# Hybrid SSD block on one core: gate weights split beside the pairs and kept as two parts, z tiles moved into a pair, rows of x loaded and scaled one by one

## The chip, the cores and the metric

The kernel runs on one core of one Trainium2 chip. The metric is device time in microseconds (us) of that core, lower is better. Engines are called by the names of the profile: PE multiplies matrices, PEld loads its weights, DVE and ACT are the vector and the scalar engine, POOL is GpSimd, SP only issues DMAs. ACT and POOL also issue DMAs, each on a queue of its own.

## The reference

One block of a streaming encoder on x of 1024 rows by 1024 channels, all float32. Cut to what matters:

```
h = rmsnorm(x) * norm_mix_w
z, xbc, dt, s_b, s_c, s_x, g_a, g_b = split(h @ w_in)     # 2048, 3072, 32, then five of 1024
xs, B, C = split(silu(causal_conv4(xbc) + bias))
y = scan over chunks of (xs, softplus(dt), A, B, C) + D * xs  # 32 heads in 4 groups
y = group_rmsnorm(y * silu(z)) * ssd_norm_w
a = y @ w_ssd_proj
b = (s_b * causal_conv3(s_c * s_x)) @ w_sconv_proj
x = x + (sigmoid(g_a) * a + sigmoid(g_b) * b) @ w_o
x = x + (silu(n @ w_gate) * (n @ w_up)) @ w_down,  n = rmsnorm(x) * norm_ffn_w
out = rmsnorm(x) * final_norm_w
```

## The kernel before, in words

**Arithmetic.** Every large product is made of three PE instructions. An operand is split into a high part (a copy by ACT into a rounded type) and a low part (a DVE subtraction of the high part from the original); then high times high, high times low and low times high are added in PSUM. One such instruction has 128 rows, 128 columns of weights and 512 columns of data. Most products are also made by a seven-product scheme (Strassen's, in Winograd's form) on halves: a `Pair` (line 834) is two slabs of w_in, 128 columns each, and its seven products each take 4 steps in depth times 3 instructions, 84 in all. A tile that is made without the scheme takes 2 halves of rows times 8 steps times 3, 48 instructions.

**Memory.** Nearly all tiles in SBUF are 47 equal pages of 128 x 1024 float32 (`page`, line 60). A page is given out again when its last user is done, and the instruction that writes it next waits for that. There are 8 PSUM banks.

**Order.** The schedule is written by hand: the order of the Python calls is the order of each engine's instructions, and every queue runs in order. Generators are advanced by one step at chosen places, so that their work lies between other work.

1. **Head** (lines 226 to 258 and 1530 to 1604). Rows of x come as eight tiles of 128 rows. Tiles 0 and 2 are loaded on SP's queue, 1 and 3 on ACT's, 4 to 7 later on ACT's (`more_loads`). Constants come on POOL's queue, and after them the first weight slabs. ACT and DVE make the sums of squares of tiles 0 to 3 in turn (`rows_sq_on`), then one norm for all four (`rstd_of`, a chain of seven small instructions, one of them on ACT), then the scaled rows in two halves of columns (`rows_scale(..., parts=2)`: DVE takes three tiles, ACT one). PE turns the scaled rows (32 transposes of 128 x 128, `turn_rows`, each group of four into one bank), ACT and DVE take the banks out (`turned_out`), `put` splits them, and `p0.pe(1)` is the first real product (line 1580). `wdt_split` and `steps_pe` make the first part of the time steps, then come the first products of two more pairs and the second half of the rows.
2. **Pairs** (lines 1641 to 1701). 31 pairs, 217 slots (a slot is one product of one pair, 12 PE instructions). A slot's evictions (`ev`), the preparation of later slots (`make`), loads about 11 slots ahead (`load_pairs`, on SP), one step of the side work (`pump`: convolutions, silu), and on every third slot a step of `all_weight_sums`, which adds blocks of later weights in DRAM with POOL's accumulating DMAs.
3. **Direct tiles beside the scans** (lines 961 to 1016). 18 tiles without the scheme: z tiles 14 and 15, and the 16 gate tiles of g_a and g_b. For each, SP loads the slab two tiles ahead, ACT makes the high part (`direct_hi`) and DVE the low part (`direct_lo`) one tile ahead. Among their PE instructions lie the 65 steps of the scan (`scans`, 32 items of two steps), spread evenly over the tiles by `turn` and `SCAN_STEPS`. The norms of y ride on the scan's steps.
4. **Two projections and the output projection** by the scheme, with chunks loaded and split ahead (`Stream`), then the **FFN**. In its `second_half` (line 1192) the turned rows of the second half are combined: two subtractions at lines 1209 and 1212, one generator step apart, each followed by the split of two pages.

The loop over the direct tiles, with the lines that the change takes out or edits:

```
for hf in range(2):
    ps = bank("pr")
    for k in range(KT):
        mm3(ps, wh[:, k, :], wl[:, k, :], bh, bl, k == 0, k == KT - 1)
        ...
        if i + 1 < len(direct) and (hf, k) == (0, 1):
            direct_hi(direct[i + 1][0])
        if i + 1 < len(direct) and (hf, k) == (0, 7):
            direct_lo(direct[i + 1][0])
        if i + 2 < len(direct) and (hf, k) == (0, 2):
            direct[i + 2][0].load()
    ev(ps, hf)
```

Of the kernel before, what the change touches and what calls it, by code (L numbers as in the profile page):

```python
# [8 lines left out]
F32 = mybir.dt.float32  # L9
# [4 lines left out]
P = 128  # L14
# [25 lines left out]
def hybrid_block(ctx: ExitStack, tc: tile.TileContext, x, nmw, w_in, cw, cb, dtb, alog, dsk, snw,  # L40
# [19 lines left out]
    def page(s, shape=(P, 1024), dt=F32):  # L60
        return pp.tile(list(shape), dt, tag="pg", name=nm(s))
# [180 lines left out]

    def more_loads(i):
        for i in (i, i + 1):
            nc.scalar.dma_start(xt[i], x[i * P:(i + 1) * P, :])
# [664 lines left out]
    z_pairs = [Pair(i * P, (silu_z(i), silu_z(i + 1))) for i in range(0, 14, 2)]  # L910
# [50 lines left out]
    z_held = []  # L961

    def z_raw(i):
        def f(ps, hf):
            if hf == 0:
                z_held.append((i, page("gt")))
            nc.scalar.activation(z_held[-1][1][:, hf * 512:hf * 512 + 512], ps, AF.Copy)
            if hf and len(z_held) == 2:
                for k, t in z_held:
                    nc.scalar.activation(t, t, AF.Silu)  # L970
                    nc.scalar.dma_start(z_d[k], t)
                z_held.clear()
        return f

    direct = [(wslab(w_in, i * P), z_raw(i)) for i in range(14, 16)]
    for j in range(KT):
        direct += [(wslab(w_in, GA0 + j * P), gate_raw(ga_d[j])), (wslab(w_in, GB0 + j * P), gate_raw(gb_d[j]))]
# [6 lines left out]

    def direct_hi(slab):
        slab.load()
        slab.hl = page("wh", slab.shape, F32R), page("wl", slab.shape, F32R)
        nc.scalar.activation(slab.hl[0], slab.st, AF.Copy)

    def direct_lo(slab):  # L990
        V.tensor_sub(slab.hl[1], slab.st, slab.hl[0].bitcast(F32))
        slab.st = None

    def direct_tile(i):
        slab, ev = direct[i]
        wh, wl = slab.hl
        slab.hl = None
# [166 lines left out]
    def ffn_phase():  # L1164
# [27 lines left out]
        def second_half(rows):  # L1192
# [19 lines left out]
            V.tensor_sub(raw0[1][1], raw0[1][1], t2[1])  # L1212
# [317 lines left out]
    a0 = rows_acc(xt[0:4], "x")  # L1530
    rows_sq_on("a", a0, "x")
    rows_sq_on("v", a0, "x")
    rows_sq_on("a", a0, "x")
    more_loads(4)
    more_loads(6)
    small_loads()
    first[1].y.load(nc.gpsimd)
    nc.gpsimd.dma_start(wdt_s, w_in[:, DT0:DT0 + H].rearrange("(k p) f -> p k f", p=P))
    first[2].y.load(nc.gpsimd)
    rows_sq_on("v", a0, "x")  # L1540
    a1 = rows_acc(xt[4:8], "x")
    del xt
    for p in first:
        p.x.load(nc.gpsimd)
    pc = bank("pc")
    nc.tensor.transpose(pc[:, 0:96], ra, ident[:96, :96])
    nc.tensor.transpose(pc[:, 96:176], rb, ident[:80, :80])
    nc.scalar.activation(cols[:, 0:176], pc[:, 0:176], AF.Copy)
    del consts, ra, rb
    r0 = rows_scale(*a0, act=(3,), parts=2)  # L1550
    raw0, raw1 = ([], []), ([], [])
    turned = {}

    def turn_rows(rows, k):
        pt = turned[k] = bank("pt")
        for i in range(4):
            nc.tensor.transpose(pt[:, i * P:(i + 1) * P], rows[i][:, k * P:(k + 1) * P], ident)
# [10 lines left out]
    p0, p1, p2 = first  # L1568
    for k in range(4):
        turn_rows(r0, k)  # L1570
    p0.hi("A1")
    turned_out(raw0, 0)
    turned_out(raw0, 1)
    turned_out(raw0, 2)
    turned_out(raw0, 3)
    p0.lo("A1")
    for k in range(4, 8):
        turn_rows(r0, k)
    every(put("B11", raw0[0]))
    p0.pe(1)  # L1580
    wdt_split()
# [22 lines left out]
    del a0, r0  # L1604
# [62 lines left out]
    sums = all_weight_sums()  # L1667
    n_slots = len(slots)
    for i in range(7 * NF, n_slots):
# [13 lines left out]
        if i % 3 == 1:  # L1683
            pump_aux()
        left = n_slots - 1 - i
# [10 lines left out]
        if left == 3:  # L1696
            direct_hi(direct[0][0])
            direct[1][0].load()
        if left == 2:
            direct_lo(direct[0][0])  # L1700
            pump_scan()
    every(sums)
    del T["T4"], b12
# [40 lines left out]
```

## Time and profile before

| What | us |
|---|---|
| median of 3 runs (1901.8 to 1903.07) | 1902.65 |
| the profiled execution | 1902.65 |
| its span, first to last instruction | 1900.8 |
| DVE busy | 1304.4 (69%) |
| ACT busy | 966.7 (51%) |
| POOL busy | 177.3 (9%) |

The profiled execution took as long as the median; 1.85 us of it lie outside the span. A row of the profile's table of groups has the line, the engine, what is written and read, the count, then the busy time in us and the mean of one in ns, then the idle time just before and what ended it. A row of the timeline has the start and the length in us. A row of the table of stages has the stage, its length, and for each engine the busy time with the count of instructions, then the granted clock of PE, the share of the DMA engines' time and GB/s. PE's matmuls overlap one another: one is listed as 0.39 us, while the next starts 0.23 us after it.

### The profile page before, as it was taken

The numbers are of one execution on the slowest core, as the hardware profiler recorded it, in microseconds if no ns is written. First come the engines' busy times: TensorE is split into PE (matmuls) and PEld (weight loads), VectorE is DVE, ScalarE is ACT, GpSimd is POOL, SyncE is SP. The second block draws the span as 40 slices with busy tenths as digits, with TensorE's granted clock in tenths as the row PEclk, the third lists the DMA queues.
The fourth block names the chain that finished last, engine by engine and source line by source line (L and its number), as shares of the span: only waits on it lengthen the run. The fifth ranks groups of instructions, "written<-read, shape, count | busy, mean of one in ns | idle before, by whom it ended". The sixth has DMA issues, their size and how long they took to land. (4 is left out here: it accounts for less than half of the span.)

```text
span 1900.8 us, 24126 instructions
## 1 busy us (share of the span) xinstructions
PE 1875.0 (99%) x8893; PEld 1541.8 (81%) x8893; DVE 1304.4 (69%) x1694; ACT 966.7 (51%) x1541; POOL 177.3 (9%) x204
## 2 busy tenths in 40 slices
PE   6999999999999999999999999999999999999998
PEld 5788888888888888888888888888888888888886
DVE  7667888778685588999978558876444444456465
ACT  5545454444443788878665454464333333335333
POOL 2010111010100000010010000102211221100000
PEclk9999999999999999999999999999999999999999
DMA  5197999978958676688899665928988888867562
GB/s 182 58 265 173 242 230 236 233 190 230 267 143 233 225 247 213 225 273 263 281 323 333 221 211 203 232 82 199 212 198 210 202 192 196 235 258 283 188 196 109
DMA packets 336150, 413.02 MB, mean 217 GB/s; under 512 B 16408, under 2 KB 217840, under 8 KB 336032
## 3 DMA queue, kind: packets, MB, share of 16 engines
q1 hardware_dynamic: 277296, 302.43, 49.0%
q0 software_dynamic: 49664, 76.27, 21.6%
q10 hardware_dynamic: 9072, 32.77, 4.3%
q8 instruction: 70, 1.15, 0.2%
q14 instruction: 48, 0.39, 0.1%
HBM read 320.56 MB, written 143.15 MB: 244 GB/s over the span
## 5 line engine op out<-in xcount | busy, mean ns | idle before, releaser
L77 DVE TENSOR_TENSOR wl<-ws,wh 128x1024 fp32r<-128x1024 f32 x77 | 94.0, 1221 | 121.6 <-ACT wh L76 121.6
L680 PE MATMUL gb<-qh,gh 128*128 128x512 f32 x432 | 168.7, 391 | 0.1
L681 PE MATMUL gb<-ql,gh 128*128 128x512 f32 x432 | 168.4, 390 | 0.0
L682 PE MATMUL gb<-qh,gl 128*128 128x512 f32 x432 | 168.3, 389 | 0.0
L682 PE MATMUL fb<-th,wl 128*128 128x512 f32 x352 | 137.2, 390 | 0.5 <-DVE wl L77 0.5
L680 PE MATMUL fb<-th,wh 128*128 128x512 f32 x352 | 137.2, 390 | 0.0
L681 PE MATMUL fb<-tl,wh 128*128 128x512 f32 x352 | 137.1, 389 | 0.0
L681 PE MATMUL gd<-ql,gh 128*128 128x512 f32 x324 | 126.3, 390 | 0.0
L680 PE MATMUL gd<-qh,gh 128*128 128x512 f32 x324 | 126.2, 389 | 0.0
L682 PE MATMUL gd<-qh,gl 128*128 128x512 f32 x324 | 126.2, 389 | 0.0
L76 ACT ACTIVATE qh<-cb 128x1024 fp32r<-128x1024 f32 x98 | 99.9, 1019 | 38.8 <-PE gb L681 17.2
L81 PE MATMUL pr<-th,wh 128*128 128x512 f32 x288 | 118.8, 413 | 0.0
L77 DVE TENSOR_TENSOR ql<-cb,qh 128x1024 fp32r<-128x1024 f32 x98 | 115.7, 1181 | 2.8 <-ACT qh L76 2.7
L83 PE MATMUL pr<-th,wl 128*128 128x512 f32 x288 | 112.8, 392 | 0.0
L82 PE MATMUL pr<-tl,wh 128*128 128x512 f32 x288 | 112.6, 391 | 0.0
L680 PE MATMUL fd<-th,wh 128*128 128x512 f32 x264 | 102.8, 389 | 0.0
L682 PE MATMUL fd<-th,wl 128*128 128x512 f32 x264 | 102.8, 389 | 0.0
L681 PE MATMUL fd<-tl,wh 128*128 128x512 f32 x264 | 102.8, 389 | 0.0
L74 DVE SCALAR_TENSOR_TENSOR gl<-ca,gh 128x1024 fp32r<-128x1024 f32 (+1 forms) x60 | 70.6, 1176 | 44.1 <-ACT gh L73 44.0
L681 PE MATMUL pb<-tl,wh 128*128 128x512 f32 x248 | 96.9, 391 | 1.9 <-DVE tl L77 1.9
L680 PE MATMUL pb<-th,wh 128*128 128x512 f32 x248 | 97.7, 394 | 0.5 <-ACT u L895 0.5
L865 ACT ACTIVATE wh<-ws 128x1024 fp32r<-128x1024 f32 x62 | 65.7, 1059 | 63.5 <-DVE ws L852 59.6
(330 smaller groups left out, 4744.4 us busy)
## 6 DMA issues: line engine op xcount, KB each, us to landing
ws<-in_w_in_dram SPq DMA_DIRECT2D x75, 512.0 KB, 5.8
ws<-in_w_gate_dram SPq DMA_DIRECT2D x77, 256.0 KB, 3.9
ws<-in_w_up_dram SPq DMA_DIRECT2D x77, 256.0 KB, 4.4
ca<-u_d SPq DMA_DIRECT2D x35, 512.0 KB, 5.2
ab<-ac_d SPq DMA_DIRECT2D x32, 512.0 KB, 5.7
xbc_g<-cv ACTq DMA_DIRECT2D x24, 512.0 KB, 6.7
ws<-ws POOLq DMA_DIRECT2D x22, 512.0 KB, 6.4
wd_d<-in_w_down_dram SPq DMA_DIRECT2D x20, 512.0 KB, 10.3
```

The lines of the kernel that those rows point to most:

```text
L74: nc.vector.scalar_tensor_tensor(lo, src, -1.0, hi.bitcast(F32), op0=ALU.mult, op1=ALU.subtract)
L76: nc.scalar.activation(hi, src, AF.Copy)
L77: nc.vector.tensor_sub(lo, src, hi.bitcast(F32))
L81: nc.tensor.matmul(o, lh, rh, start=first, stop=False)
L82: nc.tensor.matmul(o, lh, rl, start=False, stop=False)
L83: nc.tensor.matmul(o, ll, rh, start=False, stop=last)
L680: nc.tensor.matmul(o, lh, rh, start=first, stop=False, skip_group_check=True)
L681: nc.tensor.matmul(o, lh, rl, start=False, stop=False, skip_group_check=True)
L682: nc.tensor.matmul(o, ll, rh, start=False, stop=last, skip_group_check=True)
L865: nc.scalar.activation(t[0], self.source(what), AF.Copy)
```

## The change

- The two z tiles 14 and 15 become an eighth pair of z tiles, the last pair of all; `z_raw` goes. The direct tiles are the 16 gate tiles only.
- The 16 gate slabs are loaded and split beside the pairs (`gate_weights`: load, then two steps on the split, then two steps on the stores), and both parts are stored to DRAM on POOL's queue. The generator is advanced on every third slot from slot 38 on. Beside the scans, `Parts.load` fetches both parts on SP's queue; `direct_hi` and `direct_lo` go.
- In the head all eight row tiles come on SP's queue, tiles 4 to 7 each after the sum of squares of tile 0 to 3 (whose product is written into the page that the load then fills). There are two norms, one for tiles 0 and 1 and one for 2 and 3. ACT scales tiles 0 and 1 as whole rows, and PE turns them at once, tile by tile, with the turning of the constants between them. Tiles 2 and 3 are scaled in two halves; their second halves are scaled and turned after the first product. The first weight slabs come on SP's queue, after the rows.
- In the FFN both subtractions stand at the earlier place.

```diff
-    for i in range(4):
-        (nc.scalar if i % 2 else nc.sync).dma_start(xt[i], x[i * P:(i + 1) * P, :])
+    def load_x(i):
+        nc.sync.dma_start(xt[i], x[i * P:(i + 1) * P, :])
+
+    for i in range(4):
+        load_x(i)
...
-    z_pairs = [Pair(i * P, (silu_z(i), silu_z(i + 1))) for i in range(0, 14, 2)]
+    z_pairs = [Pair(i * P, (silu_z(i), silu_z(i + 1))) for i in range(0, 16, 2)]
...
+    def gate_weights():
+        for i, (c0, _) in enumerate(gates):
+            slab = wslab(w_in, c0)
+            slab.load()
+            yield
+            yield
+            hl = slab.split()
+            slab.hl = None
+            yield
+            for j in range(2):
+                nc.gpsimd.dma_start(gw_d[i][j], hl[j].bitcast(F32))
+            del hl
+            yield
...
+        def load(self):
+            if self.hl is None:
+                self.hl = page("wh", (P, KT, P), F32R), page("wl", (P, KT, P), F32R)
+                for j in range(2):
+                    nc.sync.dma_start(self.hl[j].bitcast(F32), gw_d[self.i][j])
...
-                if i + 1 < len(direct) and (hf, k) == (0, 1):
-                    direct_hi(direct[i + 1][0])
-                if i + 1 < len(direct) and (hf, k) == (0, 7):
-                    direct_lo(direct[i + 1][0])
...
-            V.tensor_sub(raw0[1][0], raw0[1][0], t2[0])
+            for k in range(2):
+                V.tensor_sub(raw0[1][k], raw0[1][k], t2[k])
             every(put("B22", raw1[1]))
             yield
-            V.tensor_sub(raw0[1][1], raw0[1][1], t2[1])
             every(put("T4", raw0[1]))
...
+    def sq_row(i):
+        t, acc = xt[4 + i], ssq[i // 2][:, i % 2:i % 2 + 1]
+        if i % 2:
+            V.scalar_tensor_tensor(t, xt[i], 1.0, xt[i], op0=ALU.mult, op1=ALU.mult, accum_out=acc)
+        else:
+            nc.scalar.activation(t, xt[i], AF.Square, accum_out=acc)
+        load_x(4 + i)
+
+    r0 = [page("xn") for _ in range(4)]
+    sq_row(0)
+    sq_row(1)
+    ra_ = rstd_of(ssq[0], D, "n")
+    sq_row(2)
+    sq_row(3)
+    first[1].y.load()
+    nc.sync.dma_start(wdt_s, w_in[:, DT0:DT0 + H].rearrange("(k p) f -> p k f", p=P))
+    first[2].y.load()
+    for p in first:
+        p.x.load()
     small_loads()
+    nc.scalar.activation(r0[0], xt[0], AF.Copy, scale=ra_[:, 0:1])
+    rb_ = rstd_of(ssq[1], D, "n")
...
+    turn_row(r0, 0, range(7))
+    pc = bank("pc")
+    nc.tensor.transpose(pc[:, 0:96], ra, ident[:96, :96])
+    nc.tensor.transpose(pc[:, 96:176], rb, ident[:80, :80])
+    nc.scalar.activation(cols[:, 0:176], pc[:, 0:176], AF.Copy)
+    del consts, ra, rb, pc
+    nc.scalar.activation(r0[1], xt[1], AF.Copy, scale=ra_[:, 1:2])
+    turn_row(r0, 1, range(7))
+    for i in range(2):
+        turn_row(r0, i, (7,))
+    for i in (2, 3):
+        V.tensor_scalar_mul(r0[i][:, lo_half], xt[i][:, lo_half], rb_[:, i - 2:i - 1])
+    p0.hi("A1")
     for k in range(4):
-        turn_rows(r0, k)
-    p0.hi("A1")
+        for i in (2, 3):
+            turn_row(r0, i, (k,))
+    for k in range(4):
+        turned_out(raw0, k)
...
     p0.pe(1)
+    V.tensor_scalar_mul(r0[2][:, hi_half], xt[2][:, hi_half], rb_[:, 0:1])
+    nc.scalar.activation(r0[3][:, hi_half], xt[3][:, hi_half], AF.Copy, scale=rb_[:, 1:2])
+    for k in range(4, 8):
+        for i in (2, 3):
+            turn_row(r0, i, (k,))
...
+        if i % 3 == 2 and i > 36:
+            next(parts, None)
...
     every(sums)
+    every(parts)
```

More of the change, by code (lines that the diff above doesn't have):

```diff
@@ L1568, in hybrid_block @@
     p0, p1, p2 = first
[L1569 to L1575 removed]
+    lo_half, hi_half = slice(0, 512), slice(512, 1024)
+    turn_row(r0, 0, range(7))
[11 more added lines that the diff above has]
+    p0.hi("A1")
+    for k in range(4):
+        for i in (2, 3):
+            turn_row(r0, i, (k,))
+    for k in range(4):
+        turned_out(raw0, k)
     p0.lo("A1")
[L1577 to L1578 removed]
     every(put("B11", raw0[0]))
     p0.pe(1)
+    V.tensor_scalar_mul(r0[2][:, hi_half], xt[2][:, hi_half], rb_[:, 0:1])
[3 more added lines that the diff above has]
+            turn_row(r0, i, (k,))
+    a1 = rows_acc(xt[4:8], "x")
+    del xt, ssq, ra_, rb_
     wdt_split()
@@ L1667, in hybrid_block @@
     sums = all_weight_sums()
+    parts = gate_weights()
     n_slots = len(slots)
```

64 lines of the change are left out of this document (15 added, 49 removed).

## The prediction

> **What bounds the kernel.** I read the page first, then the table of stages, then the waits of PE.
>
> ```profile
> span 1900.8 us, 24126 instructions
> ...
> PE 1875.0 (99%) x8893; PEld 1541.8 (81%) x8893; DVE 1304.4 (69%) x1694; ACT 966.7 (51%) x1541; POOL 177.3 (9%) x204
> ...
> PE   6999999999999999999999999999999999999998
> ...
> L680 PE MATMUL pb<-th,wh 128*128 128x512 f32 x248 | 97.7, 394 | 0.5 <-ACT u L895 0.5
> ...
> L81 PE MATMUL pr<-th,wh 128*128 128x512 f32 x288 | 118.8, 413 | 0.0
> ```
>
> ```profile
> 150.00:500.00 350.00, 349.26 (x1534) 287.21 (x1533) 267.40 (x301) 162.12 (x216) 37.87 (x43) 1.00 0.89 224
> 500.00:800.00 300.00, 299.36 (x1619) 247.07 (x1618) 224.32 (x338) 199.16 (x409) 15.87 (x21) 1.00 0.72 216
> ...
> 1500.00:1890.00 390.00, 390.00 (x1721) 322.79 (x1720) 205.35 (x248) 151.03 (x199) 28.10 (x24) 1.00 0.70 210
> ```
>
> ```profile
> PE pt L1557 <- DVE xn L137: 3.2, 3, 2.4
> PE pb L681 <- DVE tl L77: 1.9, 2, 1.1
> ...
> PE poff L476 <- ACT st L483: 0.6, 1, 0.6
> PE fb L682 <- DVE wl L77: 0.5, 1, 0.5
> ```
>
> PE is busy for 99% of the span, and "busy" alone would prove little, since its matmuls overlap. The last stage proves it: 390 us hold 1721 instructions, all of the 512-column kind, so one costs 390 / 1721 = 0.2266 us, and PE never waits for another engine there. From 150 to 800 us PE is idle for 0.74 + 0.64 = 1.4 us in 650. The longest waits stand in the first slice, where the digit is 6. So time can come from three places only: fewer PE instructions, the head, and single waits of half a microsecond. Relieving DVE, ACT or the DMAs gives nothing by itself.
>
> **The change, part by part.** *PE instructions.* The x288 of the row of `pr` on each of three lines are 864 = 18 tiles of 48. Two tiles go (96) and one pair comes (84). Net 12 fewer: 12 x 0.2266 = **-2.7 us**. The `pr` matmuls are longer in the mean (413 against 394 ns) where they follow the scan's small ones, but the scan keeps its 65 steps, so that cost stays.
>
> *The scans.* They are now spread over 768 instead of 864 matmuls; the stage loses 96 x 0.2266 = 21.8 us.
>
> ```profile
> 640.00:680.00 40.00, 39.36 (x245) 31.99 (x244) 27.06 (x48) 37.66 (x92) 0.00 (x0) 1.00 0.64 207
> 880.00:920.00 40.00, 40.00 (x254) 32.82 (x254) 38.81 (x67) 33.67 (x81) 4.70 (x7) 1.00 0.96 321
> ```
>
> ```profile
> L77 DVE TENSOR_TENSOR wl<-ws,wh 128x1024 fp32r<-128x1024 f32 x77 | 94.0, 1221 | 121.6 <-ACT wh L76 121.6
> ...
> L865 ACT ACTIVATE wh<-ws 128x1024 fp32r<-128x1024 f32 x62 | 65.7, 1059 | 63.5 <-DVE ws L852 59.6
> ```
>
> DVE is at 38.81 of 40 us late in this stage, so it could become the bound. But it is relieved of 18 low parts of 1.22 us, 22.0 us, as much as the stage gets shorter; its share stays where it is: 0. If it fell behind, one low part's time, +1.2, is my upper end. SP issues two loads in place of one, two tiles (over 30 us) ahead; 8.4 MB more over some 290 us are 29 GB/s on top of 321: covered. At the start of the stage ACT is at 37.66 of 40 and PE once waits 0.6 for it (`poff`); two z tiles' silu and the first high parts leave ACT there. I take half of that wait: **-0.3** (0 to -0.6).
>
> *The pairs* receive 16 high and 16 low parts: 17.0 us of ACT and 19.5 us of DVE over slots 38 to 221, which are 183 x 12 x 0.2266 = 498 us. From the row of 150 to 500 us, ACT goes from 46% to 50%, DVE from 76% to 80%. The extra pair brings its own splits and evictions at the same density. Traffic: per 12 slots (32.6 us) one slab in and two parts out, 1.57 MB, 48 GB/s on top of 224.
>
> ```profile
> 460.00:500.00 40.00, 40.00 (x177) 32.85 (x176) 26.47 (x31) 16.43 (x22) 6.21 (x7) 1.00 1.08 277
> ```
>
> ```profile
> ws<-in_w_in_dram SPq DMA_DIRECT2D x55, 512.0 KB, 6.0
> ```
>
> ```profile
> SPq L645 <- DVE v L644: 87.3, 8, 22.1
> ```
>
> 277 GB/s were moved there without an idle moment of PE. A slab has six slots, 16.3 us, from its issue to ACT's copy; it lands after 6.0. Queues: on SP it stands behind stores that wait for their data (`v`, up to 22.1 us) and ahead of the pairs' own slabs, which have 11 slots of lead; on ACT the copy of a slab that is late would hold the next slots' evictions; on POOL the two stores wait for the low part and stand ahead of the weight sums, which nobody needs before the projections. The added wait is not in this trace: between -1.4 (the idle time above goes) and +2.7 (PE loses one slot). The nearest rows are the single waits of 0.5 and 0.6, so I take one of them: **+0.5**.
>
> *The FFN.*
>
> ```profile
> 1298.26 2.36 DVE L77 TENSOR_TENSOR tl<-br,th 128x1024 fp32r<-128x1024 f32 x2 [0.81 <-ACT th L76]
> ...
> 1303.66 1.22 DVE L1212 TENSOR_TENSOR br<-br,t 128x1024 f32<-128x1024 f32 x1
> ```
>
> The subtraction of 1.22 us moves into a place where DVE idles 0.81; all before L1212 gets 0.4 later, all behind it 0.8 earlier, and the 0.5 us for which PE waits for the low part behind it (`fb`) goes: **-0.5** (0 to -0.5).
>
> *The head.* Here the result is decided.
>
> ```profile
> GB/s 0 53 201 410 406 404 391 364 340 244 344 389 238 271 287 357 410 373 356 381 389 385 389 184 0 0 0 0 0 0 0 0 8 0 16 0 0 0 0 287
> ```
>
> ```profile
> 5.54 1.06 ACT L117 ACTIVATE xn<-x 128x1024 f32<-128x1024 f32 x1 [2.38 <-DMA x<-in_x_dram]
> 5.72 1.22 DVE L115 SCALAR_TENSOR_TENSOR xn<-x 128x1024 f32<-128x1024 f32 x1 [4.81 <-DMA x<-in_x_dram]
> ...
> 8.72 1.22 DVE L115 SCALAR_TENSOR_TENSOR xn<-x 128x1024 f32<-128x1024 f32 x1 [1.78 <-DMA x<-in_x_dram]
> ...
> 10.07 0.20 DVE L99 TENSOR_SCALAR nv<-xss 128x4 f32<-128x4 f32 x1
> 10.19 0.32 ACT L1548 ACTIVATE cols<-pc 128x176 f32<-128x176 f32 x1 [0.69 <-PE pc L1547]
> ...
> 11.64 4.63 DVE L137 TENSOR_SCALAR xn<-x,nr 128x512 f32<-128x512 f32 x6
> ...
> 14.27 4.93 PE L1557 MATMUL pt<-ident,xn 128*128 128x128 f32 x30 [0.49 <-DVE xn L137]
> ...
> 16.19 0.74 DVE L1566 TENSOR_SCALAR br<-pt,cols 128x512 f32<-128x512 f32 x1
> ...
> 18.16 1.22 DVE L869 TENSOR_TENSOR wl<-ws,wh 128x1024 fp32r<-128x1024 f32 x1
> ...
> 20.57 0.50 PE L681 MATMUL pb<-tl,wh 128*128 128x512 f32 x1 [1.13 <-DVE tl L77]
> ...
> 23.21 0.39 PE L680 MATMUL ts<-th,wdt 128*32 128x512 f32 x1
> ...
> 32.11 1.16 ACT L135 ACTIVATE xn<-x,nr 128x1024 f32<-128x1024 f32 x1 [1.04 <-DVE nr L107]
> ```
>
> ```profile
> 14.40:17.20 2.80, 2.80 (x14) 2.80 (x15) 2.53 (x4) 1.21 (x2) 1.22 (x2) 1.00 0.93 367
> 17.40:18.90 1.50, 1.50 (x16) 1.50 (x15) 1.41 (x2) 1.47 (x2) 0.00 (x0) 1.00 1.03 355
> ```
>
> The first row is GB/s in slices of 1 us, which are also KB. Two row tiles (1049 KB) are in by 5.0 and counted as landed at 5.5. Loaded one after the other they land at 4.2, 5.5, 6.8 and 8.3: the first comes 1.3 earlier, the last 0.4. Then, step by step:
>
> - First norm: DVE's square of tile 1 from 5.6 to 7.0, the chain from 10.07 to 11.64 is 1.6, ready at 8.6. ACT's square of tile 2 stands behind the norm's root and ends at 8.7; tile 0 scaled (1.16) by 9.9.
> - The second norm starts where the only one did, since DVE's square of tile 3 waits for the first: 10.0, ready at 11.6 as before.
> - PE's transposes run at two paces: 14 in 2.8 us (0.21 each, counting whole ones) until about 17.3, 16 in 1.5 us (0.11) after. At 0.21, seven of tile 0 end at 11.4 and the constants at 12.1; `cols` (0.32) and tile 1 (1.16) follow on ACT: 13.6. Nine of tile 1: 15.6. The eight of tiles 2 and 3 (DVE's halves at 0.77 are long there, 13.2): 16.0, 16.4, 16.9, 17.3.
> - So DVE takes out its first bank at about 16.7 where it was 16.19, the low part of the weights comes at 18.25 (18.16), the second matmul at 20.6 (20.57). Splitting the norm has gained nothing: PE's slow pace and ACT's order have used it up.
> - Eight transposes that lay in PE's idle time now stand behind the first product: 8 x 0.11 = 0.9; DVE has one half more there. The time steps start at 24.0, not 23.21: **+0.8**.
>
> The ends: if all transposes run at 0.11, the steps before the first bank are 0.7 + 0.9 + 0.5 shorter, the second matmul comes at 18.4 and the time steps at 21.7, -1.5. If the slow pace lasts past the first matmuls, an estimate by the same factor of two is 1.6 more, +2.4. The Trainium skill, "TensorE: Matmul & The Clock Gate", section on the HAM clock gate, has a rule that speaks against this edit: PE runs at half rate until it has been busy through a window of about 3.4 us, and falls back after an idle one. The trace agrees (steady from 14.27, quick from about 17.3, 3.0 us), though the clock column says 1.00 throughout.
>
> Sum: -2.7 - 0.3 + 0.5 - 0.5 + 0.8 = -2.2. The profiled execution took 1902.65 like the median (span 1900.8 and 1.85 around it): **1900.5 us**.
>
> **The rivals.**
> - *Quick pace early.* PE now starts its transposes at 10.0 instead of 12.5; if the pace rises before 13.6, the head gains 1.5, and the pairs add nothing: -2.7 - 0.3 - 0.5 - 1.5 = -5.0, 1897.65. For it: more early work. Against it: PE stands idle from 12.1 to 13.6.
> - *Slow pace late.* Before, the pace rose after 3.0 us of steady work; now two idle stretches (12.1 to 13.6, 17.3 to 20.6) break that work up, and PE may stay slow through the first product: -2.7 - 0.3 + 0.5 - 0.5 + 2.4 = -0.6, 1902.05. By the Trainium skill's rule on idle windows (the section named above) it would. Against it: the wait of 1.1 us before the second matmul left the pace as it was.
> - *Late slabs hold ACT* (the slower side). If SP stands 22.1 us at a `v` store before a gate slab, the slab lands 28.1 after its place, 11.8 beyond the 16.3; ACT's copy waits, the evictions behind it too, PE has one slot (2.7) of cover, and 9.1 are lost, once: -2.7 - 0.3 + 9.1 - 0.5 + 0.8 = +6.4, 1909.05. It decides from a delay of 16.3 + 2.7 = 19.0 us on. Against it: SP's long waits are those of a queue that is ahead of the other engines.
>
> **How the numbers follow.** The forecast has 0.48, the quick pace 0.26, the slow pace 0.14, late slabs 0.12. About 0.2%, 3.8 us, can be told from no change: faster is below 1898.85, slower above 1906.45. Faster: 0.26 and 0.03 of the forecast's own spread; slower: 0.12; the rest, 0.59, within. The low end adds the quick pace, the whole 0.6 and half of the pairs' 1.4: 1896.5. The high end adds the slow pace and a lost slot and takes back the gains of the scans' start and the FFN: 1905.0. Late slabs stay outside.
>
> **What would show it.** In the changed profile: 768 `pr` matmuls with the stage about 22 us shorter; `pb` and `pd` 84 more; the first `ts` matmul near 24.0; no wait of `fb` near 1307; PE from 60 to 660 us without a wait over 1 us. A first `ts` before 22.5, or ACT's `wh` copies ended by a DMA with PE waiting for evictions, would prove me wrong.

## The result, and the profile after

The changed kernel takes 1947.72 us in the median of four runs (1944.36 to 1949.22), the kernel before 1902.42 on the same chip: the ratio is 1.0234, with a 95% interval of 1.0221 to 1.0246. It is 45 us slower. The prediction was 1900.5, in a range from 1896.5 to 1905.0: wrong, and wrong in sign. The profiled execution took 1944.36 (span 1942.6), 3.4 less than the median.

The page of the changed kernel, its first lines and PE's row of slices:

```profile
span 1942.6 us, 24330 instructions
...
PE 1889.3 (97%) x8881; PEld 1546.2 (80%) x8881; DVE 1309.6 (67%) x1707; ACT 966.9 (50%) x1544; POOL 190.1 (10%) x230
...
PE   7999999999799999999999999999999999999998
```

PE has its 12 instructions fewer, as foretold, and is idle for 53.3 us where it was for 25.8. One slice, the eleventh (486 to 534 us), shows a 7 in the middle of the pairs. The waits of PE (engine, tile and line, releaser: us in total, times, longest):

```profile
PE pt L1561 <- ACT xn L1552: 10.2, 1, 10.2
PE pb L679 <- DVE u L899: 6.9, 2, 6.3
PE poff L475 <- DVE st L484: 5.9, 2, 3.1
PE pb L679 <- ACT wh L864: 4.8, 1, 4.8
PE pd L681 <- DVE wk L868: 3.6, 2, 2.3
PE pb L681 <- DVE wl L868: 3.2, 3, 2.0
```

The first is the head. All the others are new, and they name ACT and DVE, the engines that the table of stages shows half and three quarters busy (busy us of PE, PEld, DVE, ACT, POOL; PE's clock, DMA share, GB/s):

```profile
150.00:500.00 350.00, 339.14 (x1477) 274.75 (x1475) 269.71 (x302) 164.22 (x218) 47.08 (x60) 1.00 0.96 259
500.00:800.00 300.00, 287.91 (x1460) 234.32 (x1460) 203.07 (x287) 173.09 (x346) 23.04 (x33) 0.98 0.82 247
```

To see where the time went, I compare the start of one and the same operation in two traces. The 61st `u<-u,pd` on DVE stands where the kernel before ends its pairs, the first `ab<-ab,cbm` at the first scan item, the first `h<-h,gb` well behind the scans, in the output projection. Of the differences, 19.0 (84 x 0.2266) is the added pair, and -21.8 is due in the scan stage for the two tiles that went.

| start, us | before | after | later by | of it lost |
|---|---|---|---|---|
| first `u<-u,pd` (head) | 35.4 | 37.5 | 2.1 | 2.1 |
| 61st `u<-u,pd` (pairs) | 623.5 | 655.6 | 32.1 | 30.0 |
| first `ab<-ab,cbm` | 645.5 | 696.7 | 51.2 | 0.1 |
| first `h<-h,gb` (scans, projections) | 1190.4 | 1233.3 | 42.9 | 13.5 |
| end of the span | 1900.8 | 1942.6 | 41.8 | -1.1 |

So the pairs lose 30 and the stretch from the first scan item on 13.5: 11.2 of these up to the first matmul of the projections and 2.3 behind it, where the last wait for the scans lies (1014.7 us). I call the 13.5 the scans. The head loses 2.1, and everything behind the scans gains 1.1, half of it in the FFN. A part of both large losses is not waiting but pace:

```profile
490.00:496.80 6.80, 6.61 (x30) 5.12 (x28) 3.62 (x4) 0.22 (x1) 0.00 (x0) 1.00 1.03 279
500.00:506.70 6.70, 5.22 (x11) 3.64 (x12) 4.41 (x5) 3.23 (x4) 2.09 (x3) 0.50 1.12 241
508.00:514.00 6.00, 6.00 (x28) 4.96 (x27) 2.88 (x4) 2.56 (x4) 0.87 (x1) 1.00 1.10 258
```

Behind the wait of 4.8 us the granted clock is 0.50 for 6.8 us: 11 matmuls in 5.22 us of busy time, 0.47 each, where 28 take 6.00 (0.21) a moment later. Apart from its last microseconds, the trace has five such stretches: at 500 and 524 us (6.8 each) and at 944, 981 and 1015 us (3.4 each). That is 23.8 us at half speed; by an estimate, half of it, about 12 of the 42 lost, is pace.

What stands at 500 us is best seen on ACT, with the issues of two queues beside it:

```profile
489.63 0.59 ACT L897 ACTIVATE u<-pd 128x512 f32<-128x512 f32 x1
500.33 1.06 ACT L864 ACTIVATE wh<-ws 128x1024 fp32r<-128x1024 f32 x1 [10.11 <-DMA gw_d<-wh]
...
524.06 1.06 ACT L76 ACTIVATE wh<-ws 128x1024 fp32r<-128x1024 f32 x1 [8.11 <-DMA ws<-in_w_in_dram]
```

```profile
484.23 0.89 POOL L975 DMA_DIRECT2D gw_d<-wh  x1
```

```profile
483.16 37.35 SPq L165 DMA_DIRECT2D ws<-in_w_in_dram  x4
```

A pair's high part waits 10.1 us for a page from which a gate's part, issued at 484.2, is still being stored; 24 us later a gate's high part waits 8.1 us for its slab, which was issued at 501.9. SP takes 37 us over the issues of four slabs, and the first of them alone 14.8. While ACT waits, the evictions behind it wait, and PE after them.

### The profile page after: what moved, and what is told of

It reads as the page before. It is cut to its first block, busy times and chain, and to the rows that moved or that the text cites. A ratio compares the mean times of both kernels' runs of the same rounds, so it can differ in the third digit from the quotient of the medians.

```text
span 1942.6 us, 24330 instructions
## 1 busy us (share of the span) xinstructions
PE 1889.3 (97%) x8881; PEld 1546.2 (80%) x8881; DVE 1309.6 (67%) x1707; ACT 966.9 (50%) x1544; POOL 190.1 (10%) x230
## 4 chain that ended last, share of the span: by engine, by line
PE 76%; DVE 7%; DMA 7%; issue 5%; ACT 4%; SPq 1%; POOL 0%; ACTq 0%; DVEq 0%; POOLq 0%
PE gb L679 5%; PE gb L680 5%; PE gb L681 5%; PE fb L680 4%; PE fb L681 4%; PE fb L679 4%; PE pb L681 4%; PE gd L680 4%; PE gd L681 4%; PE gd L679 4%; PE pb L679 4%; PE pb L680 4%; PE fd L680 3%; PE fd L681 3%; PE fd L679 3%
## 5 line engine op out<-in xcount | busy, mean ns | idle before, releaser
L77 DVE TENSOR_TENSOR wl<-ws,wh 128x1024 fp32r<-128x1024 f32 x93 | 113.6, 1222 | 159.5 <-ACT wh L76 155.6
L679 PE MATMUL pb<-th,wh 128*128 128x512 f32 x256 | 103.0, 402 | 8.4 <-ACT wh L864 4.8
L679 PE MATMUL pb<-th,wk 128*128 128x512 f32 x256 | 100.9, 394 | 7.2 <-DVE u L899 6.9
L864 ACT ACTIVATE wh<-ws 128x1024 fp32r<-128x1024 f32 x64 | 67.7, 1058 | 79.7 <-DVE ws L851 63.1
L76 ACT ACTIVATE wh<-ws 128x1024 fp32r<-128x1024 f32 x93 | 97.4, 1049 | 19.6 <-DMA ws<-in_w_in_dram 13.0
L81 PE MATMUL pr<-th,wh 128*128 128x512 f32 x256 | 106.3, 415 | 0.0
L681 PE MATMUL pb<-th,wl 128*128 128x512 f32 x256 | 102.4, 400 | 3.2 <-DVE wl L868 3.2
L680 PE MATMUL pb<-tl,wh 128*128 128x512 f32 x256 | 101.9, 398 | 1.8 <-DVE tl L77 1.8
```

The lines of the kernel that those rows point to most:

```text
L76: nc.scalar.activation(hi, src, AF.Copy)
L77: nc.vector.tensor_sub(lo, src, hi.bitcast(F32))
L81: nc.tensor.matmul(o, lh, rh, start=first, stop=False)
L679: nc.tensor.matmul(o, lh, rh, start=first, stop=False, skip_group_check=True)
L680: nc.tensor.matmul(o, lh, rl, start=False, stop=False, skip_group_check=True)
L681: nc.tensor.matmul(o, ll, rh, start=False, stop=last, skip_group_check=True)
```

## The experiments

Each run is compared with the kernel before on the same chip (medians 1902.4 to 1902.9). "Pairs" is how late the 61st `u<-u,pd` comes, with what the head lost; "scans" is what is lost between the first `ab` and the first `h<-h,gb`, counted as above (in e2, e8 and e15 all 18 tiles stay, so nothing is due).

| run | median | 95% interval of the ratio | pairs | scans |
|---|---|---|---|---|
| after | 1947.7 | 1.0221 to 1.0246 | 32.1 | 13.5 |
| e1_pair_ffn | 1915.2 | 1.005 to 1.008 | 0.9 | 15.8 |
| e2_head_only | 1905.2 | 1.0003 to 1.0022 | 2.9 | -0.3 |
| e3_gates_only | 1951.8 | 1.0241 to 1.0271 | 33.1 | 20.0 |
| e4_act_store | 1953.0 | 1.0244 to 1.0278 | 42.0 | 11.1 |
| e5_lead | 1947.1 | 1.0201 to 1.0258 | 34.8 | 15.2 |
| e6_no_store | 1939.7 | 1.0181 to 1.0215 | 18.9 | 16.2 |
| e7_traffic | 1915.6 | 1.005 to 1.008 | 0.9 | 15.5 |
| e8_dense | 1912.2 | 1.0033 to 1.0063 | 0.1 | 8.6 |
| e9_engines | 1925.4 | 1.0104 to 1.0134 | 10.9 | 15.4 |
| e10_no_store_lead | 1930.8 | 1.0131 to 1.0165 | 17.2 | 14.2 |
| e11_spread | 1924.6 | 1.0097 to 1.0127 | 0.0 | 22.7 |
| e12_after_spread | 1957.3 | 1.0272 to 1.0302 | 33.8 | 23.6 |
| e13_engines_act | 1915.2 | 1.005 to 1.008 | 0.9 | 15.3 |
| e14_engines_phase | 1920.0 | 1.0072 to 1.0106 | 4.3 | 16.3 |
| e15_dense_no_low | 1902.5 | 0.9992 to 1.001 | -0.6 | 0.5 |
| e16_late_parts | 1948.0 | 1.0225 to 1.0255 | 35.2 | 13.8 |
| e17_no_yt | 1938.1 | 1.0165 to 1.0204 | 34.2 | 4.6 |
| e18_pool_low | 1920.5 | 1.008 to 1.011 | 0.2 | 20.1 |

(In e11 and e12 the first scan steps lie in the pairs, so "scans" counts from the 61st `u<-u,pd`.) The last two columns are read from one profiled execution each, and that need not be a middling one: the one of e6 took 1933.8, its median is 1939.7.

**The parts of the change.** e1 takes the paired z tiles and the FFN's order, with the gates still split beside the scans:

```diff
-    z_pairs = [... for i in range(0, 14, 2)]
+    z_pairs = [... for i in range(0, 16, 2)]
-    direct = [(wslab(w_in, i * P), z_raw(i)) for i in range(14, 16)]
+    direct = []
```

> Before's head and before's splitting of gate weights beside the scans; z tiles 14 and 15 as an eighth z pair and the moved FFN subtraction are the only edits. If the loss comes from the gate parts (their pages, their DMAs, their ACT and DVE work beside the pairs), this one keeps the gains alone: 12 fewer matmuls (-2.7 us) and the FFN wait (-0.5), so 1899.2 us. Rival: the denser scans lose by themselves (DVE is at 97% there, and the changed kernel shows PE waiting for the scan's state three times after 935 us with the clock halved behind each): then about 11 us more, 1910.

e2 takes the head alone (rows of x one by one, two norms):

```diff
+    def load_x(i):
+        nc.sync.dma_start(xt[i], x[i * P:(i + 1) * P, :])
...
+    sq_row(0)
+    sq_row(1)
+    ra_ = rstd_of(ssq[0], D, "n")
```

> The new head alone, all else as before. By the changed kernel's trace its slots run 2.2 us late from the head on, so 1904.6 us. My prediction's term was +0.8 (1903.2). If the clock's free-running windows make it vary, runs should spread between about 1901 and 1905.

e3 leaves the head and the FFN as before and takes the rest of the change; e4 is e3 with the stores on ACT's queue:

```diff
-                nc.gpsimd.dma_start(gw_d[i][j], hl[j].bitcast(F32))
+                nc.scalar.dma_start(gw_d[i][j], hl[j].bitcast(F32))
```

> The z pair and the gate parts (split beside the pairs, stored by POOL, fetched beside the scans), with before's head and FFN order. If all the loss lies in the gate parts, the changed kernel's time less the head's 2.2 and plus the FFN's 0.5: about 1946 us. Rival: head and gate parts only lose together (later slots meeting other transfers): then clearly less, under 1930.

> As e3, but the two stores of each gate go out on ACT's queue, not on POOL's behind the weight sums. Theory Q (pages held by stores that stand in POOL's queue): ACT's 10 us wait for such a page near 500 us goes with what follows from it, so 12 to 20 us faster than e3. Theory L (the gate's slab lands late, since SP's loads of 512-byte rows crawl beside POOL's packets, and ACT's copy of it holds the evictions): the same traffic, within 5 us of e3, with ACT's waits for the landing of a slab still there.

The head costs 2.3 (the interval allows 0.6 to 4.2); the changed kernel's first landmark is 2.1 late. The gate parts hold the loss of the pairs (33.1 in e3, 0.9 in e1). But e1 itself loses 15.8 beside the scans, without a gate part moved; it took 1915.2 where I expected 1899.2 or 1910. And another queue for the stores gains nothing: the wait at 503 us goes, ACT waits 11.3 for a slab at 531 instead, and the pairs end 9 us later still. That the stores stand behind the weight sums in POOL's queue is not what decides.

**Late slabs, held pages, or traffic.** e5 loads each gate slab one gate tile earlier, e6 stores the first tile's parts alone, e10 does both; e7 adds to e1 only the bytes.

```diff
 e5  (the next slab is loaded before this one is split)
+            if i + 1 < len(slabs):
+                slabs[i + 1].load()
             hl = slab.split()
...
 e6
+                if i == 0:
                     nc.gpsimd.dma_start(gw_d[i][j], hl[j].bitcast(F32))
...
-                    nc.sync.dma_start(self.hl[j].bitcast(F32), gw_d[self.i][j])
+                    nc.sync.dma_start(self.hl[j].bitcast(F32), gw_d[0][j])
 e7  (in e1, every 12 slots)
+            for j in range(2):
+                nc.gpsimd.dma_start(gw_d[2 * i + j], wd[P * i:P * i + P, :])
```

> The kernel after, but each gate slab is loaded one gate tile earlier: twelve slots (32.6 us) before its split in place of six, for one page more that is held. Theory "late landing" (a slab that is loaded six slots ahead lands after its copy is due, when accumulating weight sums share the DMA engines with it, and ACT's copy holds the evictions): the waits of ACT's high part for a slab near 524 and 627 us go, the pairs' end comes at most 15 us late in place of 32, and the run takes about 1930. Rival "pages" (a page is still being stored when its next owner wants it; the slab's time has little to do with it): one more page held makes it worse or leaves it, 1947 to 1956.

> The kernel after, but only the first gate tile's two parts are stored; all sixteen tiles then load those (the gates are not the reference's). Loads, splits, matmuls and scans stay; 30 of the 32 stores of 512 KB beside the pairs are left out. Theory "stores" (their traffic and the pages that they hold cost the pairs their 30 us): the pairs' end comes at most 8 us late, the run takes 1918 to 1924. Theory "late landing" (the weight sums alone slow the gate slabs): the waits near 524 and 627 stay, 1935 to 1946. Theory "engines" (ACT's and DVE's copies are too much for the pairs): no gain, 1945 to 1949.

> The kernel with the 16 z tiles paired and the FFN's order (gates split beside the scans, 1915), with nothing added but traffic: at the places where the changed kernel stores a gate tile's parts, two copies of 512 KB from one place of DRAM to another on POOL's queue. No page, ACT or DVE takes part. If the stores hurt by their traffic alone: the pairs' end 10 us or more late, 1925 to 1940. If they hurt by the pages that they hold, or the splits do: 1914 to 1918.

> The kernel after with both cures of the pairs: only the first gate tile's parts are stored (all sixteen load those, so the gates are not the reference's), and each slab is loaded twelve slots ahead in place of six. Theory "arrivals" (each cure alone leaves the other's wait standing): no wait of ACT for a gate slab or for a stored part is left, the pairs' end comes 4 to 10 us late in place of 32, 1920 to 1928. Theory "engines": 17 us or more late still, 1935 to 1940, like the run without the stores alone.

Traffic by itself costs PE nothing. The row of 150 to 500 us of e7:

```profile
150.00:500.00 350.00, 349.26 (x1534) 287.01 (x1533) 267.38 (x301) 161.18 (x215) 47.44 (x61) 1.00 0.95 251
```

The DMA engines are as busy as in the changed kernel (0.95 against 0.96) and PE's 349.26 is that of the kernel before to the last digit. The bytes do delay something: ACT waits 6.1 us for a pair's slab at 502 us in e7, and PE does not feel it. The gate slabs, which have less lead, are not in e7. What costs is the store: without the stores 13.2 of 32.1 us come back in the trace. The wait for `gw_d<-wh` at 500 us is gone, and the waits for slabs are shorter; that the held page weighs more than the bytes is read from these waits and from e7. ACT's waits that a DMA ended between 470 and 660 us, in the changed kernel and then in e6:

```profile
ACT wh L76 <- DMA ws<-in_w_in_dram: 13.0, 2, 8.1
...
ACT wh L864 <- DMA gw_d<-wh: 10.1, 1, 10.1
```

```profile
ACT wh L76 <- DMA ws<-in_w_in_dram: 9.1, 2, 4.9
```

The late slab was the theory that I held to be the main one, and alone it fell: in e5 the two waits for slabs are gone, but with one page more in use others appear (9.6 us at 511, 4.5 at 254 and at 646, all for a stored part), and nothing is gained. With the stores gone as well (e10) the longer lead is worth 1.7 by the two traces, but 8.9 by the medians (1939.7 and 1930.8), since the trace of e6 is that of its fastest execution. So stores and late slabs together cost 15 to 17 us (14.9 in the traces, 17.0 in the medians), and how these divide is not settled. e10 has no wait for a slab or a part left, and still ends the pairs 17.2 late, where I expected 4 to 10 or, by the other theory, 17 and more with a time of 1935 to 1940. Something that is neither store nor slab was left.

**The splits themselves.** e9 adds to e1 only the splitting, of a resident page, at the change's places; e13 ACT's half of it; e14 both halves, always behind the fifth of a pair's seven slots.

```diff
 e9  (in e1, every 12 slots)
+            hl = split(T["T4"][0][0].bitcast(F32), "g", HB)
 e13 (in place of that)
+            hl = page("gh", HB, F32R)
+            nc.scalar.activation(hl, T["T4"][0][0].bitcast(F32), AF.Copy)
 e14 (where e9 splits)
-        if i % 3 == 2 and i > 36:
+        if i > 38 and (i - 21) % 7 == 4 and (i - 39) // 7 * 16 // 26 != (i - 46) // 7 * 16 // 26:
```

> The kernel with the 16 z tiles paired and the FFN's order (1915), with nothing added but the splitting: at the places where the changed kernel splits a gate slab, ACT and DVE split a page that is resident (no slab is loaded, nothing is stored, the two parts are dropped). Theory "engines" (17 us of ACT and 20 us of DVE in order ahead of evictions and operands cost the pairs their time): the pairs' end 10 us or more late, 1925 to 1945. Theory "arrivals" (what costs is that the split waits for a slab that is late or a page that is still being stored, not its length): at most 4 us late, 1915 to 1919.

> The kernel with paired z tiles and the FFN's order (1915) and, at the changed kernel's places in the pairs, only the high part of a resident page, made by ACT; no low part, no load, no store. With both parts it took 1925. If ACT's copy ahead of the evictions costs the 10 us: 1922 to 1926. If DVE's low part does: 1915 to 1917.

> The kernel with paired z tiles and the FFN's order (1915), and both parts of a resident page split 17 times beside the pairs, but always at the same place of the seven slots of a pair: the one behind which ACT is busy 20% and DVE 38% of the slot in the kernel before (elsewhere ACT up to 73%, DVE up to 99%). Every twelve slots, without regard to that, it took 1925. If the loss comes from splits that fall into slots in which DVE is full: 1915 to 1918. If the sum of the work is too much: 1923 to 1927.

The splits alone cost 10.0, ACT's copies alone nothing by the median, so it takes DVE's low part. But it is not the low part's own 1.22 us. The timeline of e9, DVE and then ACT and PE:

```profile
437.22 0.68 DVE L850 TENSOR_TENSOR ws<-ws 128x512 f32<-128x512 f32 x1
440.73 1.23 DVE L77 TENSOR_TENSOR gl<-th,gh 128x1024 fp32r<-128x1024 f32 x1 [2.83 <-ACT gh L76]
441.87 0.68 DVE L893 TENSOR_TENSOR u<-u,pd 128x512 f32<-128x512 f32 x1
442.47 0.68 DVE L869 TENSOR_TENSOR wk<-ws,wk 128x512 fp32r<-128x512 f32 x1
```

```profile
437.98 0.63 ACT L865 ACTIVATE wk<-ws 128x512 fp32r<-128x512 f32 x1 [1.26 <-DVE ws L850]
438.52 1.23 ACT L598 ACTIVATE cv<-u,cols 128x1024 f32<-128x1024 f32 x1
439.66 1.04 ACT L76 ACTIVATE gh<-th 128x1024 fp32r<-128x1024 f32 x1
```

```profile
443.21 0.50 PE L682 MATMUL pd<-th,wk 128*128 128x512 f32 x1 [1.29 <-DVE wk L869]
```

DVE has reached the low part at 437.9 and stands idle for 2.8 us, because the high part is third in ACT's queue. Behind it stand an accumulation and `wk`, a weight part for the next product, and PE waits 1.3 us for that. Each split ties DVE's queue to ACT's once more. Over the pairs, e9 and then e14 (what DVE idled before the low parts, us and times; e9 has 15 splits there, e14 has 16):

```profile
  ACT gh L76: 19.0, 12
```

```profile
  ACT gh L76: 10.4, 5
```

At a place where both engines have room the loss falls from 10.0 to 3.4, with one split more. That is 1920.0, between the two ranges that I gave, so the total alone decides nothing. Split by split the trace does. The timeline of DVE in e14, a split that waits and one that does not:

```profile
233.63 1.23 DVE L77 TENSOR_TENSOR gl<-th,gh 128x1024 fp32r<-128x1024 f32 x1 [3.12 <-ACT gh L76]
...
348.45 1.22 DVE L77 TENSOR_TENSOR gl<-th,gh 128x1024 fp32r<-128x1024 f32 x1
```

By the starts of `u<-u,pd` against e1, the pairs fall 1.3 to 1.6 us further behind at each of the three splits of e14 before which DVE idles 3.1 us (233.6, 331.3 and 447.4), and at most 0.1 at each of the ten before which it does not idle. In e9 the three splits without a wait (238.4, 371.6 and 605.1) cost at most 0.1 each as well. Of its twelve with a wait nine cost 0.6 to 3.2 and three nothing; beside the dearest, at 204.2, ACT also waits 4.6 us for a page. So what costs is the standing, though not every time, and not the 1.22 us.

**The scans.** e8 changes one number of the kernel before: the scans' steps are spread over 16 tiles in place of 18. e15 is e8 without the tiles' low parts.

```diff
 e8
-                due = turn[0] * SCAN_STEPS // (len(direct) * 2 * KT - 4)
+                due = turn[0] * SCAN_STEPS // (16 * 2 * KT - 4)
 e15 (e8, and)
-        slab.hl = page("wh", slab.shape, F32R), page("wl", slab.shape, F32R)
+        h = page("wh", slab.shape, F32R)
+        slab.hl = h, h
-        V.tensor_sub(slab.hl[1], slab.st, slab.hl[0].bitcast(F32))
```

> The kernel before, with one number changed: the scans' 65 steps are spread over the first 16 of the 18 tiles beside them, as densely as in the changed kernel, and the last two tiles run without scans. Nothing is moved otherwise. Theory "density" (the scans' chain through DVE does not keep up when a step comes every 11.7 matmuls in place of 13.1, with low parts beside them): PE waits for the scan's state late in the stage, 1909 to 1916. Rival (density costs nothing, the loss of the run with paired z tiles comes from elsewhere, such as the extra pair's leftovers): 1902 to 1904.

> The kernel before with its scans spread over the first 16 of 18 tiles (1912), and without the low parts of the 18 tiles' weights: the high part stands in for them, so the outputs are not the reference's, DVE has 22 us less and a page less is held. If the dense stage loses because DVE is full with low parts beside the scans: 1902 to 1904. If the scans' own chain can't go at a step every 11.7 matmuls: 1908 to 1913.

Density costs 8.6 with low parts and 0.5 without. The windows of 840 to 880 us, e8 and then e15, DVE in the third column of busy times:

```profile
840.00:880.00 40.00, 36.67 (x234) 30.05 (x232) 38.77 (x66) 32.97 (x82) 4.47 (x8) 0.96 0.75 239
```

```profile
840.00:880.00 40.00, 40.00 (x258) 33.22 (x257) 36.91 (x65) 35.05 (x84) 4.72 (x7) 1.00 0.87 293
```

In this window of e8 PE waits 3.3 us for the state (`poff`, 5.1 us in three waits over the stage), with half clock behind it; in e15 it does not wait. The share of DVE alone doesn't tell the two apart: the kernel before has 38.81 from 880 to 920 us, as the prediction quotes, with PE at 40.00. What tells is that the loss goes with the low parts. e15 also holds a page less, but in this stage of e8 ACT never waits for a page. e1 has the same kind of waits, 10.7 us in all, and three stretches of 3.4 us at half clock; that its loss has the same cause is taken over from e8. But the changed kernel has no low parts beside its scans, and loses 13.5. e16 loads the parts half a tile later, e17 leaves out three of the four stores of the sums that the projections read.

```diff
 e16
-                if i + 2 < len(direct) and (hf, k) == (0, 2):
+                if i + 2 < len(direct) and (hf, k) == (1, 2):
 e17
+            if f == "T1":
                 nc.gpsimd.dma_start(yt_d[f][256 * g:256 * g + 256, :]..., t)
...
-            return wfrm(yt_d, f, k, n)
+            return wfrm(yt_d, "T1", k, n)
```

> The kernel after, but the parts of the tile after next are loaded half a gate tile (5.4 us) later, so that two pages fewer are held through half of the scans. If the waits of ACT for a page of a store near 862 and 937 us set the loss of this stage: they go, and 5 to 10 us come back, 1938 to 1943. If the scans' own chain does: 1946 to 1949.

> The kernel after without three of the four stores of the sums that the projections read from DRAM (all four products read the first one's, so the outputs are not the reference's). If ACT's waits for the pages of these stores near 862 and 937 us set the 13 us that the stage loses: they go, PE's waits near 942, 981 and 1015 us with them, and 8 to 13 us come back, 1935 to 1940. If the scans' own chain does: 1945 to 1949.

e16 decides nothing: its 1948.0 is what the second theory foretold, but only the wait at 862 us went, and the one near 937 stayed (7.3). e17 took both away. ACT's wait in the changed kernel, and then all that PE waits for in the scans of e17 where the changed kernel had 5.9 for `st`:

```profile
ACT xw L440 <- DMA yt_d<-y: 9.5, 2, 6.5
```

```profile
PE prt L532 <- DVE gr L107: 1.5, 1, 1.5
PE poff L475 <- ACT st L482: 1.4, 1, 1.4
PE poff L475 <- DVE st L484: 1.3, 1, 1.3
```

8.9 of the 13.5 come back (9.6 by the medians), and the half clock at 944, 981 and 1015 us with them. So the same symptom, PE waiting for the scan's state, has two causes: low parts on DVE in e8, a page held by a store in the changed kernel.

**Attempts at a faster kernel.** e11 gives e1's scans more room, e12 the changed kernel's; e18 lets GpSimd make the low parts of e1.

```diff
 e11, e12
-    turn, SCAN_STEPS = [0, 0], 2 * G * NT + 1
+    turn, SCAN_STEPS = [0, 0], 2 * G * NT + -2 - 4
...
-        if left == 2:
+        if left in (5, 4, 3, 2):
             pump_scan()
...
-        pump_scan({1: 2, 2: 2, 4: 3}.get(ms.at, 1 if ms.at < 12 else 2))
+        pump_scan({1: 4, 2: 4, 4: 3}.get(ms.at, 1 if ms.at < 12 else 2))
 e18
-        V.tensor_sub(slab.hl[1], slab.st, slab.hl[0].bitcast(F32))
+        nc.gpsimd.tensor_sub(slab.hl[1], slab.st, slab.hl[0].bitcast(F32))
```

> The kernel with the 16 z tiles paired and the FFN's order (1915), gates split beside the scans, but the scans given more room: four steps in the last four slots of the pairs in place of one, four left to the first projections, so that beside the gates a step comes every 13.0 matmuls (before: 13.1) in place of 11.7. Theory "density": the waits for the state near 895, 951 and 986 us and the half clock behind them go, the stage loses nothing, 1899 to 1903. Rival (the stage is late for its DMAs or its pages, whatever the spacing): 1910 to 1916.

> The kernel after with the same spacing of the scans: four steps in the last slots of the pairs, four left to the projections, one every 13.0 matmuls between. Theory "density": of the 13 us that the changed kernel loses in this stage 8 or more come back, 1935 to 1940. Rival "pages" (ACT waits for a page that a store of the projections' operand still holds, and the spacing has no part in it): at most 3 us come back, 1944 to 1948.

> The kernel with the 16 z tiles paired and the FFN's order (1915), with the 16 gate tiles' low parts beside the scans made by GpSimd in place of DVE. If DVE's time with the low parts is all that makes the dense scans lose, and GpSimd's work takes nothing from DVE: 1898 to 1901, below both kernels. If GpSimd's subtraction slows DVE by as much as it relieves it: 1910 to 1916. If it is itself too slow for a tile every 10.9 us, PE waits for the low parts in every tile: 1930 or more.

All three miss. In e11 the waits near 895 us are gone as foretold, but the four steps in the last slots of the pairs make PE wait 2.9 us, and the steps left to the projections meet DVE's work there: 9.9 us of waits between 943 and 968 and 20 us at half clock. e12 does the same. In e18 DVE is relieved of 16 low parts, but GpSimd takes 2.4 us for one, and PE waits for three of them:

```profile
PE pr L83 <- POOL wl L977: 7.9, 3, 4.6
```

DVE's own work gets longer as well. One operation on DVE, e18 and then e1 (min/median/max, ns):

```profile
L449 DVE TENSOR_TENSOR ab<-ab,cbm x32: 1214/1218/3064, 664.8 to 953.0; 128x1024 f32<-128x1024 f32 x32
```

```profile
L449 DVE TENSOR_TENSOR ab<-ab,cbm x32: 1214/1216/1226, 665.4 to 946.4; 128x1024 f32<-128x1024 f32 x32
```

Of the 32, 25 are as quick as ever and seven take 1.7 to 3.1 us, as if DVE were shut out at times and not slowed throughout. The Trainium skill, "SBUF — State Buffer", section "SBUF: two separate sides", says that a DVE operation with two inputs in SBUF and a GpSimd operation that reads SBUF lock each other out for a whole instruction; the two rows agree. No kernel here beats the one before.

## Why the prediction was wrong, point by point

- *PE instructions, -2.7.* Right: the page counts x8881 where it counted x8893, 768 of them `pr`, and `pb` and `pd` 84 more.
- *The FFN, -0.5.* Right: the wait of `fb` is gone and the stretch gains 0.6.
- *The head, +0.8.* The rival "slow pace late" came, at the price that it was given: it was to cost 2.4 and costs 2.1 in the changed kernel, 2.3 alone. That the price fits is in part luck: the time steps start at 26.29, later than the rival's 25.6 (24.0 and 1.6), and 1.0 is made up before the first `u<-u,pd`. The timeline of PE, changed kernel:

```profile
13.68 3.89 PE L1561 MATMUL pt<-ident,xn 128*128 128x128 f32 x17 [1.44 <-ACT xn L1584]
18.86 0.79 PE L679 MATMUL pb<-th,wh 128*128 128x512 f32 x1 [1.29 <-ACT th L76]
20.68 0.80 PE L680 MATMUL pb<-tl,wh 128*128 128x512 f32 x1 [1.02 <-DVE tl L77]
21.27 0.63 PE L681 MATMUL pb<-th,wl 128*128 128x512 f32 x1
...
25.11 0.55 PE L681 MATMUL pb<-th,wl 128*128 128x512 f32 x1
25.50 0.71 PE L1561 MATMUL pt<-ident,xn 128*128 128x128 f32 x5
```

  The second matmul starts at 20.68 (20.6 was forecast), but the ten from 21.27 to 25.11 follow each other by 0.427 us, not 0.2266: the broken-up start left PE at half pace through the first product. The clock column still says 1.00 there, as it did before; in e17, which has the same head, it shows the half:

```profile
21.20:24.40 3.20, 3.20 (x9) 2.32 (x8) 3.20 (x7) 2.09 (x5) 0.00 (x0) 0.50 0.95 284
```

  The steps up to the second matmul were right, and the weight of 0.14 on this rival too small.
- *The pairs, +0.5.* This step failed, by 29.5 of the 47 us. It went wrong in three places. First, "ACT goes from 46% to 50%, DVE from 76% to 80%": a share over 350 us says nothing of queues that go in order. The cost lay in DVE standing idle before the low part (e9: 19.0 us of it, and 10.0 us lost; e13: no low part, and no loss). A hint stood in a row that the prediction quotes for the 1.22 us: behind the bar it has 121.6 us of idleness for 77 low parts, 1.6 each, all ended by ACT's high part. Those 77 stand behind the pairs, where PE waited for a low part of weights once, 0.5 us (`fb`); the row tells the standing, not its price. In the changed kernel that row reads

```profile
L77 DVE TENSOR_TENSOR wl<-ws,wh 128x1024 fp32r<-128x1024 f32 x93 | 113.6, 1222 | 159.5 <-ACT wh L76 155.6
```

  and 16 low parts more brought 37.9 us of it; in the pairs DVE idled 28.8 us before 12 of the 15 that lie there, 2.4 each. Second, "the two stores wait for the low part and stand ahead of the weight sums, which nobody needs": I asked who waits for the queue, not who waits for the pages that the stores hold. Without the stores 13.2 came back (8.1 by the medians), with the longer lead as well 14.9 (17.0). Third, "277 GB/s were moved there without an idle moment of PE" is true, and e7 confirms it, but it bounded traffic, which was not the cost. The remaining 5.1 (17.2 of e10 less 2.1 for the head and 10.0 for the splits) isn't taken apart.
- *The rival "late slabs hold ACT", 1909.05, 0.12.* Its second half is in the trace (ACT waits 8.1 and 4.9 us for slabs), but not its trigger: SP did not stand at a `v` store, its issues and the transfers were slow (the slab of 524.0 was issued at 501.9). It was priced as one event of 9.1. Waits came for pages too, and half clock followed each of the two long ones. As a cause by itself it fell in e5; next to the stores it has a share of 2 to 9 us.
- *The scans, -0.3.* It failed by 13.8. The argument that DVE is relieved "as much as the stage gets shorter" is borne out: e15 loses 0.5 at that density without low parts. What I missed is that ACT may ask for a page which a store of the projections' sums still holds: 8.9 of the 13.5, shown by e17. Why it does so here and not before stays open: the slowest of these stores between 900 and 1000 us lands after 12.8 us where it was 9.4, but the medians are alike (8.0 and 8.2), and e16, with fewer pages in use, kept the wait. The other 4.6 are about the three waits left in e17, 4.2 us where the kernel before has 0.9; what they come from isn't taken apart.
- *The rest of the 47.* 29.5 + 13.8 + 1.3 for the head - 0.6 behind the scans make 44.0; the profiled execution lies 3.4 below the median.
- *The signs.* Of what would show it, the counts and the missing wait of `fb` came. The first `ts` came at 26.29, not near 24.0; the stage of the `pr` matmuls got 10.5 us shorter, not 22; and between 60 and 660 us PE had six waits over 1 us, up to 6.3. The sign of being wrong that was named, ACT's `wh` copies ended by a DMA with PE waiting behind them, is what stands at 500 and 524 us.
- *Two slips in the working.* The low end's own terms give 1896.65, not 1896.5, and the slices put the fourth row tile at 8.1, not 8.3. Nothing hangs on either.

## What to carry to other kernels

Before moving work "beside" a stage, ask of each added instruction what stands behind it in its queue and on whom it waits: a split on two in-order engines ties both queues together, and here its price was the standing (1.3 to 1.6 us where DVE idled 3.1), not its 1.2 us. An added store costs the time for which its buffer is not free, so count buffers from issue to landing, not bytes per second. And when PE is the bound, a wait can cost more than its length: here those of 2.9 to 6.3 us had 3.4 or 6.8 us at half clock behind them, by an estimate 1.7 to 3.4 us more.

## What the runs showed of the hardware

The clock falls behind waits shorter than its own window. In the changed kernel waits of 1.5 us (at 1014.7) to 6.3 us were followed by 3.4 or 6.8 us at a granted clock of 0.50. In e11 a wait of 2.8 us at 943.4 was followed by 3.4, and two of 4.0 and 3.1 us, 5 us apart, stand in a stretch of 17:

```profile
962.00:979.00 17.00, 13.44 (x62) 11.23 (x63) 15.62 (x28) 3.32 (x6) 1.45 (x2) 0.50 0.62 227
```

The Trainium skill, "TensorE: Matmul & The Clock Gate", section on the HAM clock gate, gives windows of about 3.4 us, which the lengths bear out, and says that an idle window brings the clock down; here 1.5 us of idleness were once enough, and 2.3 us at 210.9 were not.

An issue on SP can take long: 14.8 us for one slab at 483 us. By itself that did no harm: the kernel before has issues of 14.6 and 13.0 us at 470 and 490 us and no wait of PE behind them.
